# A two-layer attention trunk on one core: value products for two pairs of heads at a time, and up products grouped by the rounded and the remainder part of the weights

## The chip, the core and the metric

The kernel runs on one core of a Trainium2 chip. A core has engines that work side by side and each take their instructions in a fixed order: TensorE (PE in the profile, with its weight loads as PEld), VectorE (DVE), ScalarE (ACT), GpSimd (POOL, unused here but for a few instructions) and SyncE (SP), which issues the DMA transfers from HBM. Matmul results go to PSUM, which has eight banks of 512 float32 columns on each of 128 partitions; VectorE and ScalarE read them from there. The metric is the time of one execution in device microseconds, the median of several runs.

## The reference

Two layers work on 256 tokens of width 1024. Each layer is a mixer and an MLP, both between norms:

```
h   = rms_norm(x, g_pre_mix);  parts = h @ w_in
o   = concat(nsa(parts), fox(parts));  x += rms_norm(o @ w_out, g_post_mix)
h   = rms_norm(x, g_pre_mlp)
y   = square(relu(h @ w_up)) @ w_down;  x += rms_norm(y, g_post_mlp)
```

`nsa` has 8 query heads in 2 groups that share keys and values. Each head has three outputs (compressed, selected and window attention), and their gated sum is its result. At 256 tokens all blocks are selected and the window covers everything before the token, so selected and window attention are both causal softmax attention, over different keys and values. Compressed attention has 15 keys, made from the tokens by a small network. `fox` has 8 heads of causal softmax attention with a forgetting term added to the logits. All of it is float32.

## The kernel before

**Products in three parts.** TensorE multiplies a rounded float32 type faster than full float32. Each weight that arrives from HBM (`wraw`) is split into a rounded part `whi` (ScalarE) and a remainder `wlo` (VectorE), and activations are split in the same way. A product then is `hi*hi + hi*lo + lo*hi`, three matmuls into the same PSUM columns (`mm3`). Softmax probabilities and values stay in full float32, and so do transposes.

**An order made by a planner.** Almost all instructions are recorded first (`Recorder`), so that they have one source line in the profile, L350, where they are emitted. The planner (`order`, from line 243) then plays the recording with costs for each operation and decides in which order each engine takes its work: the one with the lowest key that is ready, where keys follow the order of recording. A group inside `nc.stretch()` stays together on TensorE. Buffers are part of this: an operation whose tile has no free buffer waits, and tiles of one tag get theirs in the order of recording. The order is fixed when the program is built; on the chip each engine follows it and waits on semaphores.

**The mixer.** The columns of `w_in` are computed in six chunks (c0 to c5). Attention runs in a loop over `flat` (lines 1237 to 1273): 16 steps for NSA (four pairs of heads, two heads a pair, selected and window branch) and 8 for fox. In this pipeline each iteration does the scores of step i (TensorE, then on VectorE the mask and row extremes, on ScalarE the exponentials), scales those of step i-1 (`scale`, VectorE), transposes those of step i-2 (`probs_T`: three TensorE transposes into a PSUM bank of tag "s" and a copy to the tile `prT`, by VectorE and ScalarE in turn), and multiplies with the values what was ready at step i-3 (`pv`). Between these, `fill` takes pieces of a stream of other TensorE work: the chunks c1 to c5, then the products with `w_out` of the first four 128-row slices.

**Value products.** `pv` runs once for each pair of heads, when both heads (and, for NSA, both branches) are there: 4 NSA pairs and 4 fox pairs in a layer. For a pair it has a PSUM bank of tag "o" (there is one), of which it uses 256 columns; one head's output goes to partitions 0 to 63, the other's to 64 to 127. Each matmul has 64 columns of values as weights, so two run beside each other in two halves of the array. NSA has two terms (selected `vS`, window `vW`), fox has one (`fV`). For NSA a full-width matmul adds the compressed branch of the pair (`vbig`, `pcT`). `o_evac` then splits the 256 columns into the rounded and remainder tiles `oT` (tags act0 and act1, two buffers each, which the MLP uses for its activations).

**The MLP.** The hidden width of 4096 is worked on in 8 slices of 512. The first (`up0`) is computed by tokens. The other seven (`up`, line 1319) are computed transposed in four blocks of 128 hidden rows: 8 steps over the input width with, in each, a 512-wide matmul of `whi` with both parts of `xT` side by side and a 256-wide matmul of `wlo` with the rounded part, which is added to the upper 256 columns. Two layers of seven slices of four blocks make 56 blocks. Each slice is followed by the down products of the slice before it, into four PSUM banks (tags "x" and "acc").

The functions that the diff touches:

Of the kernel before, what the change touches and what calls it, by code (L numbers as in the profile page):

```python
# [18 lines left out]
F32 = mybir.dt.float32  # L19
# [5 lines left out]
P = 128  # L25
D = 1024
S = 256
NT = 2
DEPTH = 2
HD = 64  # L30
# [430 lines left out]
def trunk(nc, A, consts_in, out, sbp, pp):  # L461
    def tile(shape, dtype, name, tag=None, bufs=1):
        return nc.tile(sbp[(tag or name) not in OPERANDS], shape, dtype, name, tag, bufs)

    def psum(tag):
        return nc.tile(pp, [P, 512], F32, tag, tag, {"acc": 2, "x": 2, "s": 3, "o": 1}[tag], psum=True)

    def small(shape, name, bufs=2):
        return tile(shape, F32, name=name, tag=name, bufs=bufs)
# [18 lines left out]
    for l in range(DEPTH):  # L488
        w_in = A["w_in"][l].rearrange("(k p) n -> p k n", p=P)
        for c, (a, b) in enumerate(CHUNKS):  # L490
            for q, (k0, k1) in enumerate(parts_of(l, c)):
                add_unit((l, "in", c, q), [k1 - k0, b - a], w_in[:, k0:k1, a:b])
                if (c, q) in RIDES:
                    s, j = RIDES[c, q]
# [24 lines left out]
    def weight(*key):  # L519
        return W.get(index[key])  # L520
# [55 lines left out]
    def load_gains(*rows):  # L576
        g = tile([P, 2, D], F32, name="gains", tag="gain")
        for i, (name, l) in enumerate(rows):
            nc.sync.dma_start(g[:, i, :], A[name][l].partition_broadcast(P))
        return [g[:, i, :] for i in range(2)]  # L580
# [23 lines left out]
    def split(src, dst):  # L604
        nc.scalar.activation(dst[0], src, AF.Copy)
        nc.vector.tensor_sub(dst[1], src, dst[0].bitcast(F32))
# [123 lines left out]
    for l in range(DEPTH):  # L730
# [12 lines left out]
        vS, vW, fV, gate = ([None] * 2 for _ in range(4))  # L743
        gates = small([P, NT, 24], "gate")
        T = {}
        oT = {}
# [301 lines left out]
        done = set()  # L1048
# [23 lines left out]
        def fill(n):  # L1072
            for _ in range(n):
                if step() in ("wait", "end"):
                    return
# [33 lines left out]
        def scores(e):  # L1109
            kind, pair, par, br = e[:4]  # L1110
            if kind == "fox":
                if par == 0:
                    T["sc"] = fox_scores(pair)
                ps = T["sc"][par]
            else:
                if br == 1:
                    T["sc"] = nsa_scores(e)
                ps = T["sc"][br - 1]
            p = small([P, 384], "pr", 3)
            st = small([P, 4], "st", 4)  # L1120
            for a, b, t in SEGS:
                nc.vector.tensor_tensor_reduce(
                    out=p[:, a:b], in0=ps[t], in1=cst[:, C_MASK + 256 - (b - a):C_MASK + 256], op0=OP.add, op1=OP.min,
                    scale=-0.125, scalar=3.0e38, accum_out=st[:, t:t + 1])
            for a, b, t in SEGS:
                nc.scalar.activation(p[:, a:b], p[:, a:b], AF.Exp, scale=-1.0, bias=st[:, t:t + 1],
                                     accum_out=st[:, 2 + t:3 + t])
            return p, st

        def scale(e, p, st):  # L1130
            kind, pair, par, br = e[:4]
            nc.vector.reciprocal(st[:, 2:4], st[:, 2:4])
            for a, b, t in SEGS:
                if kind == "fox":
                    nc.vector.tensor_scalar(p[:, a:b], p[:, a:b], st[:, 2 + t:3 + t], None, op0=OP.mult)
                else:
                    c = 3 * (2 * pair + par) + br
                    nc.vector.tensor_scalar(p[:, a:b], p[:, a:b], st[:, 2 + t:3 + t], gate[t][:, c:c + 1],
                                            op0=OP.mult, op1=OP.mult)

        def probs_T(p, eng):
            ps = psum("s")
            for a in (0, 128, 256):
                nc.tensor.transpose(ps[:, a:a + P], p[:, a:a + P], ident)
            pT = small([P, 384], "prT", 6)
            if eng:
                nc.scalar.activation(pT, ps[:, :384], AF.Copy)
            else:
                nc.vector.tensor_copy(pT, ps[:, :384])
            return pT  # L1150

        def pv(o, terms, last):

            with nc.stretch():
                for i, (pT, V, cols) in enumerate(terms):
                    for kb in range(2):
                        for par in range(2):
                            h = slice(par * HD, par * HD + HD)
                            c = cols[par]
                            if kb == 0:  # L1160
                                nc.tensor.matmul(o[h, 0:S], V[0][:, c:c + HD], pT[par][:, 0:S],
                                                 start=i == 0, stop=False, skip_group_check=True)
                            else:
                                nc.tensor.matmul(o[h, P:S], V[1][:, c:c + HD], pT[par][:, S:S + P],
                                                 start=False, stop=last and i == len(terms) - 1, skip_group_check=True)

        def o_evac(o, kind, pair):
            if (kind, 0) not in oT:
                for j in range(2):
                    oT[kind, j] = tile([P, 4, S], F32R, name="oT", tag=f"act{j}", bufs=2)  # L1170
            split(o[:, :S], [oT[kind, j][:, pair, :] for j in range(2)])
            done.add(("o", pair + (0 if kind == "nsa" else 4)))


        if first:
# [61 lines left out]
        flat = [("nsa", pair, par, br) for pair in range(4) for par in range(2) for br in (1, 2)]  # L1237
# [4 lines left out]
        st = {}  # L1242
        pTs = {}
        o = None
        nc.lane = len(nc.ops)
        for i in range(len(flat) + 4):
            if 0 <= i - 1 < len(flat):
                scale(flat[i - 1], *st[i - 1])
            if i < len(flat):
                st[i] = scores(flat[i])  # L1250
                if i == 15:
                    done.add("nsa")
                    g_post, g_pre2 = load_gains(("g_post_mix", l), ("g_pre_mlp", l))
            fill(1)
            if i in side:
                side[i]()
                fill(1)
            if 0 <= i - 2 < len(flat):
                pTs[flat[i - 2]] = probs_T(st.pop(i - 2)[0], i % 2)
            fill(1)  # L1260
            j = i - 3
            if 0 <= j < len(flat) and flat[j][2] == 1 and flat[j][3] != 1:
                kind, pair, par, br = flat[j]
                o = psum("o")
                cols = [(pair // 2) * HD] * 2 if br else [2 * pair * HD, 2 * pair * HD + HD]
                pv(o, [([pTs.pop((kind, pair, x, b)) for x in range(2)], (fV, vS, vW)[b], cols)
                       for b in ((1, 2) if br else (0,))], not br)
                if br:
                    nc.tensor.matmul(o[:, :S], T["vbig"][:, pair].rearrange("p j d -> p (j d)"), T["pcT"],
                                     start=False, stop=True, skip_group_check=True)  # L1270
                o_evac(o, kind, pair)
            if i >= 12 or i % 2:
                fill(1)

# [44 lines left out]
        def up(fc, then=None):  # L1319
            a = [tile([P, 4, S], F32R, name="aT", tag=f"act{j}", bufs=2) for j in range(2)]  # L1320
            for b in range(4):
                hi, lo = weight(l, "up", fc, b)

                ps = psum("s")
                for k in range(8):
                    nc.tensor.matmul(ps, hi[:, k, :], xT[2][:, k].rearrange("p j n -> p (j n)"), start=k == 0, stop=False,
                                     skip_group_check=True)
                    nc.tensor.matmul(ps[:, S:], lo[:, k, :], xT[0][:, k, :], start=False, stop=k == 7,
                                     skip_group_check=True)
                if then is not None and b == 1:  # L1330
                    then()
                if b % 2 == 0:
                    h = tokt("h")
                d = h[:, (b % 2) * S:(b % 2) * S + S]
                nc.scalar.activation(d, ps[:, S:], AF.Copy)
                nc.vector.tensor_add(d, ps[:, :S], d)
                if b % 2:
                    rl = small([P, 512], "rl")
                    nc.scalar.activation(rl, h, AF.Relu)
                    nc.vector.tensor_mul(h, rl, rl)  # L1340
                    d = [y[:, b - 1:b + 1, :].rearrange("p b n -> p (b n)") for y in a]
                    nc.scalar.activation(d[0], rl, AF.Square)
                    nc.vector.tensor_sub(d[1], h, d[0].bitcast(F32))
            return a
# [41 lines left out]
        act, then = up0()  # L1386
        for fc in range(8):
# [12 lines left out]
            if fc < 7:  # L1400
# [5 lines left out]
                act = nxt  # L1406
# [59 lines left out]
```

## Time and profile before

| | |
|---|---|
| median of 3 runs | 635.33 us (635.32 to 635.46) |
| the profiled execution | 635.77 us, of which the span of instructions is 634.0 us |
| PE busy | 625.5 us (99%), 3570 matmuls |
| PEld busy (weight loads) | 520.4 us (82%) |
| DVE busy | 480.9 us (76%) |
| ACT busy | 373.8 us (59%) |
| granted clock of TensorE | 0.998 |
| HBM read | 114.07 MB |

Attention lies at about 56 to 126 us in the first layer and 368 to 437 us in the second; the seven transposed up slices and their down products fill most of the time between 150 and 315 us and between 460 and 615 us. In the page, a group of instructions has its engine, its operation, the tiles it writes and reads, its shape, how often it occurs, its busy time, and the mean length of one in ns. Matmuls overlap with the next, so their length is more than their share of the time; the distance from one start to the next is that share. In the timeline, neighbouring instructions of one group are merged into one row with a count.

### The profile page before, as it was taken

Reading aid. Unit: us, or ns where it says so; the run is one execution under the profiler, and the core shown is the slowest. Engines: PE = TensorE matmul, PEld = TensorE weight load, DVE = VectorE, ACT = ScalarE, POOL = GpSimd, SP = SyncE. Lnnn points to the kernel's source line nnn. Section 1 sums busy time; section 2 is a strip of 40 time slices with the busy share of each in tenths; the row PEclk is TensorE's granted clock in tenths of the full one; section 3 lists DMA queues with packets and bytes.
Section 4 is the critical chain, followed back from the end, with each engine's and each line's share of the span. In section 5 each row is a group of like instructions: output and inputs, shape, how many; then the busy total and the mean of one; then the engine's idle time right before and its main releaser. Section 6 shows DMA issues by size and latency. Waiting matters only on the chain.

```text
span 634.0 us, 9913 instructions
## 1 busy us (share of the span) xinstructions
PE 625.5 (99%) x3570; PEld 520.4 (82%) x3570; DVE 480.9 (76%) x1084; ACT 373.8 (59%) x737; POOL 0.2 (0%) x4
## 2 busy tenths in 40 slices
PE   9999999999999999999999999999999999999995
PEld 6888977688888888888888988777888888888884
DVE  6899998869985665566598999987998665666544
ACT  7865676564864455456467656864658464455432
POOL 0000000000000000000000000000000000000000
PEclk9999999999999999999999999999999999999999
DMA  8998436225786666656329954432267766655601
GB/s 307 345 321 284 131 100 168 85 67 174 247 280 196 196 178 197 194 185 183 121 81 308 331 167 130 166 101 67 66 230 259 228 184 197 197 184 186 197 1 66
DMA packets 47005, 115.75 MB, mean 183 GB/s; under 512 B 4003, under 2 KB 14573, under 8 KB 46957
## 3 DMA queue, kind: packets, MB, share of 16 engines
q1 hardware_dynamic: 46956, 115.13, 56.8%
q8 instruction: 28, 0.46, 0.3%
q14 instruction: 21, 0.16, 0.1%
HBM read 114.07 MB, written 1.05 MB: 182 GB/s over the span
## 4 chain that ended last, share of the span: by engine, by line
PE 98%; DMA 1%; DVE 0%; ACT 0%; SPq 0%; issue 0%; DVEq 0%
PE s L350 35%; PE acc L350 31%; PE x L350 25%; PE o L350 7%; DMA wraw<-in_w_in_dram 1%; SPq L350 0%; DVE x L350 0%; DVE m L350 0%; DVEq L1462 0%; ACT whi L350 0%; ACT xT L350 0%; DVE rsqrt L350 0%; ACT rl L350 0%; DVEq L350 0%
## 5 line engine op out<-in xcount | busy, mean ns | idle before, releaser
L350 DVE TENSOR_TENSOR wlo<-wraw,whi 128x1024 fp32r<-128x1024 f32 (+2 forms) x196 | 230.2, 1180 | 101.8 <-ACT whi L350 100.1
L350 ACT ACTIVATE whi<-wraw 128x1024 fp32r<-128x1024 f32 (+2 forms) x196 | 199.7, 1025 | 157.0 <-PE acc L350 74.2
L350 PE MATMUL s<-xT,whi 128*128 128x512 f32 x448 | 158.5, 397 | 0.0
L350 PE MATMUL s<-xT,wlo 128*128 128x256 f32 x448 | 125.7, 281 | 0.0
L350 PEld LDWEIGHTS s<-xT,whi 128*128 128x128 f32 x448 | 84.1, 188 | 20.5
L350 PE MATMUL acc<-whi,aT 128*128 128x512 f32 x256 | 88.9, 391 | 0.0
L350 PE MATMUL x<-whi,aT 128*128 128x512 f32 x256 | 88.8, 391 | 0.0
L350 PEld LDWEIGHTS s<-xT,wlo 128*128 128x128 f32 x448 | 84.6, 189 | 0.6
L350 PEld LDWEIGHTS x<-whi,aT 128*128 128x128 f32 x256 | 47.9, 188 | 10.2
L350 PEld LDWEIGHTS acc<-whi,aT 128*128 128x128 f32 x256 | 48.0, 188 | 10.0
L350 ACT ACTIVATE pr<-pr,st 128x128 f32<-128x128 f32 (+1 forms) x96 | 42.8, 447 | 17.5 <-DVE st L350 17.1
L350 PE MATMUL acc<-wlo,aT 128*128 128x512 f32 x128 | 49.9, 390 | 0.0
L350 PE MATMUL x<-wlo,aT 128*128 128x512 f32 x128 | 49.9, 390 | 0.0
L350 PE MATMUL acc<-xT,whi 128*128 128x256 f32 x256 | 49.4, 285 | 0.0
L350 PEld LDWEIGHTS acc<-xT,whi 128*128 128x128 f32 x256 | 40.4, 190 | 2.3 <-issue 1.4
L350 PE MATMUL x<-whi,xT 128*128 128x512 f32 x112 | 37.9, 408 | 0.5 <-ACT whi L350 0.3
L350 PE MATMUL acc<-whi,xT 128*128 128x512 f32 (+1 forms) x128 | 38.2, 359 | 0.0
L350 PE MATMUL acc<-xT,wlo 128*128 128x256 f32 x128 | 36.3, 286 | 0.0
L350 ACT ACTIVATE rl<-x 128x512 f32<-128x512 f32 x24 | 14.7, 612 | 24.9 <-PE x L350 16.8
L350 PEld LDWEIGHTS acc<-wlo,aT 128*128 128x128 f32 x128 | 24.0, 188 | 5.1
L350 PEld LDWEIGHTS x<-wlo,aT 128*128 128x128 f32 x128 | 24.0, 188 | 4.6
L350 ACT ACTIVATE h<-s 128x256 f32<-128x256 f32 x56 | 20.6, 368 | 10.7 <-PE s L350 10.7
(219 smaller groups left out, 963.2 us busy)
## 6 DMA issues: line engine op xcount, KB each, us to landing
wraw<-in_w_up_dram SPq DMA_DIRECT2D x64, 512.0 KB, 3.7
wraw<-in_w_down_dram SPq DMA_DIRECT2D x64, 512.0 KB, 3.9
wraw<-in_w_in_dram SPq DMA_DIRECT2D x39, 512.0 KB, 5.0
wraw<-in_w_out_dram SPq DMA_DIRECT2D x16, 512.0 KB, 3.6
w<-in_cmp_w_k_dram SPq DMA_DIRECT2D x8, 512.0 KB, 5.4
w<-in_cmp_w_v_dram SPq DMA_DIRECT2D x8, 512.0 KB, 8.2
wraw<-in_w_in_dram SPq DMA_DIRECT2D x8, 288.0 KB, 5.1
x<-in_x_dram SPq DMA_DIRECT2D x4, 256.0 KB, 7.4
```

What stands on the lines that cost most here:

```text
L350: getattr(getattr(self.nc, op.engine), name)(*[real(v) for v in args], **{k: real(v) for k, v in kw.items()})
```

## The change

Two edits that don't touch each other.

Value products: `pv` now takes two pairs. At the even pair nothing is done; at the odd pair one group holds the matmuls of both, the even pair in columns 0 to 255 of the bank, the odd pair in columns 256 to 511, and only the first matmul of each partition half clears the bank. The two `vbig` matmuls follow it, and one evacuation of 512 columns fills two slices of `oT`. The even pair's `prT` tiles are thus held until the odd pair is ready; for the odd NSA pairs the transposed probabilities go to a new tile `prX` in the buffers of tags act0 and act1.

Up products: in each block the eight 512-wide matmuls with `whi` come first, then the eight 256-wide ones with `wlo`; the number and the operands are the same.

```diff
-        def probs_T(p, eng):
+        def probs_T(p, eng, e):
             ps = psum("s")
             for a in (0, 128, 256):
                 nc.tensor.transpose(ps[:, a:a + P], p[:, a:a + P], ident)
-            pT = small([P, 384], "prT", 6)
+            kind, pair, par, br = e
+            if kind == "nsa" and pair % 2:
+                if br == 1:
+                    T["prX"] = tile([P, 4, S], F32, name="prX", tag=f"act{par}", bufs=2).rearrange("p b n -> p (b n)")
+                pT = T["prX"][:, (br - 1) * 384:br * 384]
+            else:
+                pT = small([P, 384], "prT", 6)
...
-        def pv(o, terms, last):
+        def pv(o, pairs, last):
             with nc.stretch():
-                for i, (pT, V, cols) in enumerate(terms):
+                for q, terms in enumerate(pairs):
+                    for i, (pT, V, cols) in enumerate(terms):
...
-                                nc.tensor.matmul(o[h, 0:S], V[0][:, c:c + HD], pT[par][:, 0:S],
-                                                 start=i == 0, stop=False, skip_group_check=True)
+                                    nc.tensor.matmul(o[h, q * S:q * S + S], V[0][:, c:c + HD], pT[par][:, 0:S],
+                                                     start=q == 0 and i == 0, stop=False, skip_group_check=True)
...
-            split(o[:, :S], [oT[kind, j][:, pair, :] for j in range(2)])
+            split(o.rearrange("p (b n) -> p b n", b=2), [oT[kind, j][:, pair - 1:pair + 1, :] for j in range(2)])
...
-                o = psum("o")
...
+                if pair % 2:
+                    o = psum("o")
...
+                    if br:
+                        for q in range(2):
+                            nc.tensor.matmul(o[:, q * S:q * S + S], T["vbig"][:, pair - 1 + q].rearrange("p j d -> p (j d)"),
+                                             T["pcT"], start=False, stop=True, skip_group_check=True)
+                    o_evac(o, kind, pair)
...
                 for k in range(8):
                     nc.tensor.matmul(ps, hi[:, k, :], xT[2][:, k].rearrange("p j n -> p (j n)"), start=k == 0, stop=False,
                                      skip_group_check=True)
+                for k in range(8):
                     nc.tensor.matmul(ps[:, S:], lo[:, k, :], xT[0][:, k, :], start=False, stop=k == 7,
                                      skip_group_check=True)
```

More of the change, by code (lines that the diff above doesn't have):

```diff
@@ L1150, in probs_T @@
             return pT
-        def pv(o, terms, last):
+        def pv(o, pairs, last):
             with nc.stretch():
-                for i, (pT, V, cols) in enumerate(terms):
[L1156 to L1160, printed above, removed]
-                                nc.tensor.matmul(o[h, 0:S], V[0][:, c:c + HD], pT[par][:, 0:S],
-                                                 start=i == 0, stop=False, skip_group_check=True)
-                            else:
-                                nc.tensor.matmul(o[h, P:S], V[1][:, c:c + HD], pT[par][:, S:S + P],
-                                                 start=False, stop=last and i == len(terms) - 1, skip_group_check=True)
+                for q, terms in enumerate(pairs):
+                    for i, (pT, V, cols) in enumerate(terms):
+                        for kb in range(2):
+                            for par in range(2):
+                                h = slice(par * HD, par * HD + HD)
+                                c = cols[par]
+                                if kb == 0:
+                                    nc.tensor.matmul(o[h, q * S:q * S + S], V[0][:, c:c + HD], pT[par][:, 0:S],
+                                                     start=q == 0 and i == 0, stop=False, skip_group_check=True)
+                                else:
+                                    nc.tensor.matmul(o[h, q * S + P:q * S + S], V[1][:, c:c + HD], pT[par][:, S:S + P],
+                                                     start=False, stop=last and i == len(terms) - 1,
+                                                     skip_group_check=True)
         def o_evac(o, kind, pair):
@@ L1170, in o_evac @@
                     oT[kind, j] = tile([P, 4, S], F32R, name="oT", tag=f"act{j}", bufs=2)
-            split(o[:, :S], [oT[kind, j][:, pair, :] for j in range(2)])
-            done.add(("o", pair + (0 if kind == "nsa" else 4)))
+            split(o.rearrange("p (b n) -> p b n", b=2), [oT[kind, j][:, pair - 1:pair + 1, :] for j in range(2)])
+            for x in (pair - 1, pair):
+                done.add(("o", x + (0 if kind == "nsa" else 4)))
         if first:
@@ L1258, in trunk @@
             if 0 <= i - 2 < len(flat):
-                pTs[flat[i - 2]] = probs_T(st.pop(i - 2)[0], i % 2)
+                pTs[flat[i - 2]] = probs_T(st.pop(i - 2)[0], i % 2, flat[i - 2])
             fill(1)
@@ L1263, in trunk @@
                 kind, pair, par, br = flat[j]
-                o = psum("o")
[L1265 to L1271, printed above, removed]
+                if pair % 2:
+                    o = psum("o")
+                    cols = lambda q: [(q // 2) * HD] * 2 if br else [2 * q * HD, 2 * q * HD + HD]
+                    pv(o, [[([pTs.pop((kind, q, x, b)) for x in range(2)], (fV, vS, vW)[b], cols(q))
+                            for b in ((1, 2) if br else (0,))] for q in (pair - 1, pair)], not br)
+                    if br:
[3 more added lines that the diff above has]
+                    o_evac(o, kind, pair)
             if i >= 12 or i % 2:
```

## The prediction

> **What bounds the kernel now.** I read the page first (share of each engine, chain of work), then the view of waits for TensorE alone, then the timeline of TensorE in the stages that the change touches.
>
> ```profile
> span 634.0 us, 9913 instructions
> ...
> PE 625.5 (99%) x3570; PEld 520.4 (82%) x3570; DVE 480.9 (76%) x1084; ACT 373.8 (59%) x737; POOL 0.2 (0%) x4
> ...
> PE 98%; DMA 1%; DVE 0%; ACT 0%; SPq 0%; issue 0%; DVEq 0%
> ...
> L350 PE MATMUL s<-xT,wlo 128*128 128x256 f32 x448 | 125.7, 281 | 0.0
> ...
> L350 PEld LDWEIGHTS s<-xT,wlo 128*128 128x128 f32 x448 | 84.6, 189 | 0.6
> ```
>
> ```profile
> PE o L350 <- DVE warm L350: 1.2, 1, 1.2
> PE x L350 <- ACT whi L350: 0.3, 1, 0.3
> PE x L350 <- ACT xT L350: 0.2, 1, 0.2
> ```
>
> TensorE (PE) carries 98% of the chain that ends last, and the second fence is everything it waited for: 1.7 us of 634. So the time is the sum of the distances from one matmul's start to the next one's. A busy figure does not give that distance, because matmuls overlap (281 ns "of one" in the group row is longer than its slot); the timeline does. Whatever the change takes out of those distances comes off the end, unless PE must then wait for something.
>
> **Change 1, the order in the up products.** Each of 56 blocks (28 a layer; 448 / 8) has eight 512-wide matmuls on rounded weights and eight 256-wide on remainders. They alternate now; after the change eight of one kind precede eight of the other. Nothing is added or removed. The rows are TensorE's timeline (start, length, operation, how many were merged): a stretch of down products with 512 columns alone, then four alternating up blocks.
>
> ```profile
> 495.41 0.40 PE L350 MATMUL acc<-whi,aT 128*128 128x512 f32 x1
> ...
> 504.95 0.39 PE L350 MATMUL s<-xT,whi 128*128 128x512 f32 x1
> 505.17 0.28 PE L350 MATMUL s<-xT,wlo 128*128 128x256 f32 x1
> 505.29 0.40 PE L350 MATMUL s<-xT,whi 128*128 128x512 f32 x1
> ...
> 516.24 0.40 PE L350 MATMUL x<-whi,aT 128*128 128x512 f32 x1
> ```
>
> From 495.41 to 504.95 there are 42 matmuls of 512 columns: 9.54 / 42 = 0.2271 us each. From 504.95 to 516.24 there are 32 alternating pairs: 11.29 / 32 = 0.3528 us a pair. The price of 256 columns among their own kind is in the forget-query products of layer 0, where only such matmuls follow each other:
>
> ```profile
> 63.83 0.40 PE L350 MATMUL acc<-xT,whi 128*128 128x256 f32 x2
> ...
> 65.63 0.63 PE L350 MATMUL x<-kx,qS 128*128 128x512 f32 x2
> ...
> 66.10 0.39 PE L350 MATMUL acc<-xT,whi 128*128 128x256 f32 x2
> ...
> 68.83 0.29 PE L350 MATMUL acc<-xT,wlo 128*128 128x256 f32 x1
> ```
>
> Fifteen steps in 1.80 us and 23 in 2.73: 4.53 / 38 = 0.1192 us. So a pair costs 0.3528 - 0.2271 - 0.1192 = 0.0065 us more in alternation than its two parts do apart: the price of two changes of width. A block keeps one such pair of changes and loses seven: 7 x 0.0065 x 56 = 2.5 us. Every weight is needed at the same time as now or later: the block starts on rounded weights, which are one tile and are already all needed at its first matmul, and the remainders, which VectorE (DVE) makes, are first read eight matmuls in, not one. I therefore add no wait. The bounds of this part: a gain of 2.5 if the slots are as quoted; a loss if remainders in a row are paced by their weight loads, whose row says 189 ns: 7 x (0.189 - 0.119) x 56 = 27 us lost. I take the first, because the 256-wide stream above loads weights for each matmul too and still steps at 0.119.
>
> **Change 2, probabilities times values for two pairs at once.** Now there are 16 groups of such products (8 a layer), each holding PE in a mode with 64 output columns; after, 8 groups of double length. The matmuls in them are the same in number and size. What goes is eight changes into the mode and eight out of it. One NSA group (two terms a pair) and one forget group (one term):
>
> ```profile
> 72.81 0.63 PE L350 MATMUL x<-kx,qS 128*128 128x512 f32 x2
> 73.37 0.87 PE L350 MATMUL o<-prT,vS 128*64 128x256 f32 x8
> 74.07 0.82 PE L350 MATMUL o<-prT,vW 128*64 128x256 f32 x8
> 74.82 0.50 PE L350 MATMUL acc<-xT,whi 128*128 128x256 f32 x2
> 75.16 0.28 PE L350 MATMUL acc<-xT,wlo 128*128 128x256 f32 x1
> ```
>
> ```profile
> 125.42 0.39 PE L350 MATMUL x<-whi,oT 128*128 128x512 f32 x1
> 125.74 0.87 PE L350 MATMUL o<-prT,fV 128*64 128x256 f32 x8
> 126.54 0.50 PE L350 MATMUL x<-whi,oT 128*128 128x512 f32 x1
> 126.88 0.40 PE L350 MATMUL x<-wlo,oT 128*128 128x512 f32 x1
> ```
>
> Two terms take 74.82 - 73.37 = 1.45 us, one takes 126.54 - 125.74 = 0.80, so a term alone is 0.65 and 0.15 of each group is fixed. The matmul before it is late in giving way: 73.37 - 72.81 = 0.56 for two that cost 0.454 elsewhere (0.10), 0.32 instead of 0.227 (0.09). The one after it as well: 0.34 for two 256-wide ones that cost 0.238 (0.10), 126.88 - 126.54 = 0.34 instead of 0.227 (0.11). Together 0.15 + 0.10 + 0.10 = 0.35 us a group; eight groups fewer give 2.8 us.
>
> The product of compressed probabilities (o<-pcT,vbig) follows each NSA pair, eight in all. In the built order before, three of them stand between rounded-type matmuls; after, all eight stand as four twos behind transposes of probabilities, which are of the same unrounded type.
>
> ```profile
> 93.66 0.48 PE L350 MATMUL acc<-wlo,xT 128*128 128x512 f32 x1
> 93.97 0.59 PE L350 MATMUL o<-pcT,vbig 128*128 128x256 f32 x2
> ```
>
> The step into one is 0.31 instead of 0.227: 0.09 each, three times, 0.3 us.
>
> Evacuation of the outputs: 16 of 256 columns become 8 of 512 on ScalarE (ACT) and on DVE. The groups by form give the sizes:
>
> ```profile
> L350 DVE TENSOR_TENSOR oT<-o,oT 128x256 fp32r<-128x256 f32 x16 | 6.7, 419 | 2.2 <-ACT oT L350 2.2
> L350 ACT ACTIVATE oT<-o 128x256 fp32r<-128x256 f32 x16 | 6.0, 374 | 7.0 <-PE o L350 7.0
> L350 DVE TENSOR_TENSOR xT<-s,xT 128x512 fp32r<-128x512 f32 x12 | 8.2, 691 | 2.6 <-ACT xT L350 2.5
> L350 ACT ACTIVATE xT<-s 128x512 fp32r<-128x512 f32 x12 | 7.1, 598 | 4.1 <-PE s L350 3.9
> ```
>
> By the xT rows of the same form, DVE saves 6.7 - 8 x 0.691 = 1.2 us and ACT 6.0 - 8 x 0.598 = 1.2 us. Both lie beside PE and I count nothing. One evacuation lasts longer (0.598 + 0.691 = 1.29 us against 0.79), which matters behind the last group of a layer, where out products of its pairs follow. In the built order four other matmuls (0.9 us) stand between that group and the first that needs its rounded part, so I cost this at nothing; with the cover gone it costs at most 0.5 us a layer.
>
> What is queued behind the long group: while PE does 2 x 1.3 + 0.15 = 2.75 us of value products it makes no scores and no transposes, which DVE lives on. The stages of layer 0 (PE busy, PEld, DVE, ACT, with counts):
>
> ```profile
> 70.00:84.00 14.00, 14.00 (x101) 11.76 (x99) 13.57 (x61) 9.86 (x31) 0.00 (x0) 1.00 0.28 95
> 84.00:98.00 14.00, 14.00 (x97) 10.53 (x95) 13.53 (x54) 10.69 (x36) 0.00 (x0) 1.00 0.51 142
> 98.00:112.00 14.00, 14.00 (x86) 10.32 (x85) 11.23 (x38) 9.27 (x25) 0.00 (x0) 1.00 0.54 162
> ```
>
> DVE has 0.43 and 0.47 us to spare in 14 where the NSA pairs run and 2.77 in the next stage. The new order fills the long groups with splits of weights on DVE (wlo), which have to be done anyway, so I cost this at zero; the loss end is the longer hold itself: 1.30 us at four NSA groups and 0.65 at four forget groups, 7.8 us.
>
> The odd pairs' transposed probabilities go to a new tile in the act0 and act1 buffers. The copies keep their size and engine; these buffers are unused by then in layer 0, and in layer 1 their readers, the last down products of layer 0, are long past. On SP's queue of loads one step moves: in layer 0 the two gain loads, issued at 91.77, come behind one more load of out weights and one of up weights.
>
> ```profile
> 91.77 0.33 SPq L350 DMA_DIRECT2D gains<-in_g_post_mix_dram  x1
> ...
> 94.38 0.33 SPq L350 DMA_DIRECT2D wraw<-in_w_out_dram  x1
> 97.84 40.80 SPq L350 DMA_DIRECT2D wraw<-in_w_up_dram  x8
> ```
>
> At worst they go out after the first of the loads from 97.84, six microseconds late, while their first reader on DVE stands 12 instructions further on (12 x 13.53 / 54 = 3 us), so it would wait 3 us; at best they go out when they do now, since the two loads ahead wait for weight splits that the new order puts earlier. I take zero, as PE has fill matmuls for such a gap. Nothing moves on POOL.
>
> **The sum.** -2.5 - 2.8 - 0.3 = -5.6 us. The profiled execution took 635.77 us (span 634.0 and 1.8 around it): 630.2. Its time is 0.44 above the median of the runs, so the median should come to 635.33 - 5.6 = 629.7 us.
>
> **The rivals.** *Order does not matter:* the 6.5 ns belong to the up products themselves (their operands), not to the change of width, and stay. For it: the price is a difference of three rows from three places. Against it: the operands are laid out as in those rows. Then only change 2 pays: 635.33 - 3.1 = 632.2. The Trainium skill ("TensorE: Matmul & The Clock Gate", section "Back-to-back issue gap") has such a rule for the plain matmul: a gap of N / 2.4 + 2.5 ns, whatever stands beside it. By it a pair would cost 325 ns in either order and change 1 would give nothing; the trace has 352.8, so the rule does not hold to the 7 ns in question here.
>
> *DVE runs dry (slower):* each long group delays scores and transposes, DVE falls behind by the longer hold, and PE, once its fill is used up, waits for transposed probabilities. Place: the matmuls right behind each double group. Price: up to 7.8 us, 635.33 - 5.6 + 7.8 = 637.5. It decides once 70% of the hold comes back as PE waits (5.6 of 7.8). For it: the DVE rows at 97%. Against it: the weight splits that fill the gap, and the 2.77 us of the next stage. Half of it would give 633.6.
>
> *Remainders paced by their loads (slower):* 27 - 3.1 is 24 us more, 659. It decides from a slot of 0.119 + 5.6 / 392 = 0.133 us for a 256-wide matmul in a row (392 = 7 x 56). For it: 189 ns a load, and that in the 256-wide stream two of three matmuls reload the same weights. Against it: the third does not, and no step there stands out.
>
> **How the numbers follow.** The sum as worked out 0.60 (its own range 628.4 to 631.2: half a microsecond of late evacuation a layer above, 1.3 us of better slots below). Order does not matter 0.12. DVE dry by half 0.06, by about all of the gain (no change) 0.07, beyond it 0.11. Loads 0.04. A measurement of this kernel can tell about 0.2% (1.3 us) from no change. Faster: 0.60 + 0.12 + 0.06 = 0.78; same 0.07; slower 0.15. The range 627.6 to 635.4 holds the first three and most of the fourth; below it reaches 0.8 us past the first's own range for a dearer mode change than the two groups shown.
>
> **What would show it.** In the profile after: the up blocks at 8 x 0.227 + 8 x 0.119 + 0.007 = 2.78 us where four took 11.29 (2.82 each); eight groups in the 64-column mode, NSA ones near 2.75 us and forget ones near 1.45; the view of PE's waits still under 3 us. A PE wait for prT, prX or pr behind a double group shows the second rival; a 256-wide step over 0.133 us shows the third; up blocks still at 2.82 show the first. The prediction is wrong if PE waits for more than 4 us in the attention stages, or if the long groups cost more inside than their terms.

## The result, and the profile after

The changed kernel takes 630.87 us (median of 4 runs, 630.74 to 631.18) against 635.39 for the kernel before beside it (635.32 to 635.72): a ratio of 0.9928, 95% interval 0.9914 to 0.9942. That is 4.5 us less, where 5.6 were forecast; the time lies inside both ranges of the prediction.

From the page of the changed kernel (span, busy time of the engines, shares of the chain, one group: busy us, mean ns of one, idle before), and from its view of TensorE's waits (engine and tile, what it waited for, us in total, times, longest):

```profile
span 629.0 us, 9910 instructions
...
PE 619.7 (99%) x3570; PEld 521.0 (83%) x3570; DVE 480.8 (76%) x1076; ACT 373.4 (59%) x729; POOL 0.2 (0%) x4
...
PE 95%; DVE 1%; ACT 1%; DMA 1%; SPq 0%; issue 0%; DVEq 0%; ACTq 0%
...
L350 PE MATMUL s<-xT,wlo 128*128 128x256 f32 x448 | 62.5, 282 | 0.0
```

```profile
PE o L350 <- DVE warm L350: 1.2, 1, 1.2
PE acc L350 <- DVE fkT L350: 0.5, 1, 0.5
PE x L350 <- ACT whi L350: 0.4, 1, 0.4
PE x L350 <- ACT xT L350: 0.2, 1, 0.2
```

TensorE is still the chain (95%) and waits for 2.3 us in all. Two things are to be seen. The group of narrow up matmuls fell from 125.7 us busy to 62.5 with the same 448 matmuls, while the whole kernel gained 4.5: a group's busy time counts overlap with its neighbours, so regrouping halves it and says nothing of a gain. And one wait is new: `acc` for DVE's `fkT`.

Where the time went is read from the starts of three matmuls: the first wide one of the up products of layer 0, the first of layer 1 (288 columns) and the first wide up matmul of layer 1. TensorE's timeline of before, then of after:

```profile
149.44 0.39 PE L350 MATMUL s<-xT,whi 128*128 128x512 f32 x1
...
329.74 0.29 PE L350 MATMUL acc<-whi,xT 128*128 128x288 f32 x1
...
460.20 0.39 PE L350 MATMUL s<-xT,whi 128*128 128x512 f32 x1
```

```profile
147.43 1.98 PE L350 MATMUL s<-xT,whi 128*128 128x512 f32 x8
...
326.65 0.29 PE L350 MATMUL acc<-whi,xT 128*128 128x288 f32 x1
...
456.27 1.98 PE L350 MATMUL s<-xT,whi 128*128 128x512 f32 x8
```

With the first 288-column matmul of layer 0 (17.83 us before, 17.68 after) and the span's end, these cut the span into four stages, the ruler for everything below. A row is one profiled execution; a stage is the difference of two starts in us:

| kernel | mixer of layer 0 | MLP of layer 0 | mixer of layer 1 | MLP of layer 1 to the end |
|---|---|---|---|---|
| before | 131.62 | 180.30 | 130.46 | 173.78 |
| changed | 129.75 | 179.21 | 129.63 | 172.69 |
| up products alone | 131.36 | 179.21 | 130.49 | 172.69 |
| value products alone | 129.63 | 180.29 | 129.64 | 173.91 |
| compressed product between | 130.87 | 179.24 | 130.53 | 172.71 |
| early bank | 129.16 | 179.23 | 129.05 | 172.69 |
| four and four | 129.77 | 179.75 | 129.62 | 173.19 |
| zigzag | 129.72 | 179.21 | 129.91 | 172.68 |
| forget pairs alone in twos | 130.63 | 179.22 | 129.80 | 172.69 |
| NSA pairs alone in twos | 130.29 | 179.23 | 130.68 | 172.68 |
| changed, again | 129.72 | 179.22 | 129.61 | 172.70 |
| early bank, again | 129.62 | 179.22 | 129.19 | 172.68 |
| zigzag and early bank | 129.78 | 179.22 | 129.05 | 172.68 |

The MLP stages repeat within 0.03 us among kernels with the same up order (0.13 in the second one of before's order; more on it under change 1 below). The mixer of layer 0 does not: the early bank gives 129.16 and 129.62 in two executions, and 129.78 with the zigzag, where TensorE also waits 0.37 us for a load. So changed less before is -1.87 and -0.83 in the mixers and -1.09 and -1.09 in the MLPs, -4.88 together; the rest of the 5.0 between the spans lies ahead of the first of these matmuls.

### The profile page after: what moved, and what is told of

It is laid out like the page before. It is cut to its first block, busy times and chain, and to the rows that moved or that the text cites. A ratio compares the mean times of both kernels' runs of the same rounds, so it can differ in the third digit from the quotient of the medians.

```text
span 629.0 us, 9910 instructions
## 1 busy us (share of the span) xinstructions
PE 619.7 (99%) x3570; PEld 521.0 (83%) x3570; DVE 480.8 (76%) x1076; ACT 373.4 (59%) x729; POOL 0.2 (0%) x4
## 4 chain that ended last, share of the span: by engine, by line
PE 95%; DVE 1%; ACT 1%; DMA 1%; SPq 0%; issue 0%; DVEq 0%; ACTq 0%
PE s L350 35%; PE acc L350 30%; PE x L350 23%; PE o L350 7%; DMA wraw<-in_w_in_dram 1%; ACT whi L350 0%; SPq L350 0%; ACT rl L350 0%; DVE wlo L350 0%; ACT xT L350 0%; DVE pr L350 0%; DVE fkT L350 0%; DVE x L350 0%; DVE m L350 0%; DVEq L1476 0%
## 5 line engine op out<-in xcount | busy, mean ns | idle before, releaser
L350 PE MATMUL s<-xT,whi 128*128 128x512 f32 x448 | 112.0, 392 | 0.0
L350 PEld LDWEIGHTS s<-xT,whi 128*128 128x128 f32 x448 | 81.4, 189 | 15.2
L350 PEld LDWEIGHTS s<-xT,wlo 128*128 128x128 f32 x448 | 61.1, 190 | 4.4
L350 PE MATMUL s<-xT,wlo 128*128 128x256 f32 x448 | 62.5, 282 | 0.0
L350 PE MATMUL acc<-whi,xT 128*128 128x512 f32 (+1 forms) x128 | 36.2, 355 | 0.5 <-DVE fkT L350 0.5
L350 ACT ACTIVATE rl<-h 128x512 f32<-128x512 f32 x28 | 17.4, 623 | 16.1 <-DVE h L350 16.1
```

Of the source, the lines that this page charges most:

```text
L350: getattr(getattr(self.nc, op.engine), name)(*[real(v) for v in args], **{k: real(v) for k, v in kw.items()})
```

## The experiments

Each ratio is to the kernel before, run beside it; the median of before was 635.56 us for the first four below; 635.39 for the changed kernel and the early bank side by side and for the NSA pairs alone; and 635.72 for the other four.

### Each edit alone

The up products alone, on the kernel before:

```diff
                 for k in range(8):
                     nc.tensor.matmul(ps, hi[:, k, :], ...)
+                for k in range(8):
                     nc.tensor.matmul(ps[:, S:], lo[:, k, :], ...)
```

> The kernel before with the grouped up products alone. Theory A (the two edits add up; the landmarks of the two MLPs moved by -1.06 us each): 2.1 us below before, 633.3, up blocks at 2.79 us each. Theory B (the prediction's term): 2.5 us below, 632.9, blocks at 2.78. Theory C (order does not matter, the gain in the MLP came with the value products): within 0.3 us of before, blocks at 2.82.

Measured: 633.29 us, ratio 0.9965 (0.9952 to 0.9977), 2.3 us less. The table has -1.09 in each MLP and nothing in the mixer of layer 1, 2.2 us in all: nearest to theory A; theory C falls. (B's 2.5 lies inside the interval too; it is the table that speaks against it. The 0.26 us in the mixer of layer 0, which the edit doesn't touch, is within what that stage varies.)

The value products alone, from the changed kernel:

```diff
-                for k in range(8):
                     nc.tensor.matmul(ps[:, S:], lo[:, k, :], ...)
```

> The changed kernel with the alternating order of up products put back, so the double value groups alone. Theory A (what the traces show for the two attention stages): 2.4 us below before, 633.0, with about 0.8 us of PE lost behind the evacuation fkT of the fourth chunk. Theory B (the prediction's term): 3.1 us below, 632.3. Theory C (all of the gain is from the value products): 4.5 us below, 630.9.

Measured: 633.39 us, ratio 0.9966 (0.9953 to 0.9978), 2.2 us less; in the table -1.99 and -0.82 in the mixers, nothing gained in the MLPs. That is nearest to theory A, and C falls: each edit gains in its own stage, the two add up (2.3 + 2.2 = 4.5), and neither brings it all. B's 3.1 lies just outside the interval (about 1.4 to 3.0).

### What a way into the 64-column mode and out of it costs

The order is changed so that each NSA double group is left once in its middle, for a product that is there anyway and is of the same unrounded type:

```diff
                                     nc.tensor.matmul(o[h, q * S + P:q * S + S], V[1][:, c:c + HD], ...)
+                    if not last:
+                        nc.tensor.matmul(o[:, q * S:q * S + S], T["vbig"][:, vpair - 1 + q]..., T["pcT"], ...)
...
-                        for q in range(2):
-                            nc.tensor.matmul(o[:, q * S:q * S + S], T["vbig"][:, pair - 1 + q]..., T["pcT"], ...)
```

> The changed kernel, but in each of the four NSA double groups the compressed product of a pair comes right behind that pair's selected and window products, so PE leaves the 64-column mode and enters it again once more in the middle of each group; all matmuls the same. Theory A (a way into the mode and out of it costs 0.35 us, whatever stands between): 4 x 0.35 = 1.4 us above the changed kernel. Rival (the price belongs to the change between rounded and unrounded operands, which the compressed product does not have): within 0.3 us of the changed kernel.

Measured: 632.99 us, ratio 0.9959 (0.9946 to 0.9971): 2.6 us below before where the changed kernel is 4.5 below, so about 1.9 above it. TensorE's timeline of the changed kernel around one NSA double group and one forget group, then of this one around an NSA double group:

```profile
85.22 0.87 PE L350 MATMUL o<-prT,vS 128*64 128x256 f32 x8
85.92 0.82 PE L350 MATMUL o<-prT,vW 128*64 128x256 f32 x8
86.57 0.82 PE L350 MATMUL o<-prX,vS 128*64 128x256 f32 x8
...
87.97 0.44 PE L350 MATMUL s<-cst,pr 128*128 128x128 f32 x2
88.24 1.03 PE L350 MATMUL o<-pcT,vbig 128*128 128x256 f32 x4
89.11 0.49 PE L350 MATMUL s<-cst,pr 128*128 128x128 f32 x3
...
114.84 1.52 PE L350 MATMUL o<-prT,fV 128*64 128x256 f32 x16
116.30 0.50 PE L350 MATMUL acc<-whi,oT 128*128 128x512 f32 x1
```

```profile
396.75 0.82 PE L350 MATMUL o<-prT,vW 128*64 128x256 f32 x8
397.50 0.70 PE L350 MATMUL o<-pcT,vbig 128*128 128x256 f32 x2
398.13 0.87 PE L350 MATMUL o<-prX,vS 128*64 128x256 f32 x8
398.83 0.82 PE L350 MATMUL o<-prX,vW 128*64 128x256 f32 x8
399.58 0.70 PE L350 MATMUL o<-pcT,vbig 128*128 128x256 f32 x2
400.11 0.71 PE L350 MATMUL s<-cst,pr 128*128 128x128 f32 x5
```

In the undisturbed group the second term steps in 86.57 - 85.92 = 0.65 us, and the compressed products take 89.11 - 88.24 = 0.87 for two. Left in the middle, the term ahead takes 0.75 (396.75 to 397.50), the compressed product 0.63 instead of 0.43, and the first term of the second pair 0.70 instead of 0.65: 0.10 + 0.20 + 0.05 = 0.35 us, the price in the prediction, with no change of operand type in it. So the rival falls: the 64-column mode has this price. (The Trainium skill, "TensorEngine Tiling (Array Packing)", section "Key Properties", says that a change of tiling mode drains the engine and gives no price; the 0.35 us in and out are in keeping with it, though no row shows the draining itself.) At the group's end the compressed product loses 0.10 where transposes had lost 0.05, so a group costs 0.39 more and four 1.6; the remaining 0.3 us (0.5 by the two mixers of the table, 1.1 and 0.9 longer) came with an order that differs at other places too, and was not followed up.

### The evacuation that lost its cover

In the changed kernel TensorE's timeline has this at the start of chunk c5, in layer 0 and in layer 1; below it DVE's timeline in layer 1:

```profile
74.07 0.28 PE L350 MATMUL acc<-xT,wlo 128*128 128x256 f32 x1
74.42 0.50 PE L350 MATMUL acc<-whi,xT 128*128 128x512 f32 x1
...
382.77 0.28 PE L350 MATMUL acc<-xT,wlo 128*128 128x256 f32 x1
383.50 0.50 PE L350 MATMUL acc<-whi,xT 128*128 128x512 f32 x1 [0.46 <-DVE fkT L350]
```

```profile
381.64 1.21 DVE L350 TENSOR_TENSOR wlo<-wraw,whi 128x1024 fp32r<-128x1024 f32 x1
382.76 1.29 DVE L350 TENSOR_TENSOR fkT<-acc,rT 128x512 f32<-128x512 f32 x2
```

The steps are 0.35 and 0.73 us where 0.12 is usual. The first bank of c4 must be evacuated (`fkT`) before c5 writes into it, and DVE reaches that only after a split of weights. In the kernel before, the value products of the first NSA pair stood between the last matmuls of c4 and covered it (TensorE's timeline, then DVE's, of before):

```profile
385.59 0.87 PE L350 MATMUL o<-prT,vS 128*64 128x256 f32 x8
...
387.04 0.39 PE L350 MATMUL acc<-xT,wlo 128*128 128x256 f32 x1
...
387.50 0.28 PE L350 MATMUL acc<-xT,wlo 128*128 128x256 f32 x1
387.62 0.40 PE L350 MATMUL acc<-whi,xT 128*128 128x512 f32 x1
```

```profile
385.85 0.68 DVE L350 TENSOR_TENSOR fkT<-acc,rT 128x512 f32<-128x512 f32 x1
```

The group ran from 385.59 to 387.04, `fkT` at 385.85 beside it, and c5 followed after 0.12 us. To test this, the cover is made unnecessary: the last part of c3's and c4's products finishes the first bank before it turns to the second.

```diff
-                for k in range(k0, k1):
-                    for b in range(4):
+                for k, b in ([(k, b) for b2 in (0, 2) for k in range(k0, k1) for b in (b2, b2 + 1)] if k1 == 8 else
+                             [(k, b) for k in range(k0, k1) for b in range(4)]):
```

> The changed kernel, but the last part of the chunk products of c3 and c4 finishes the first PSUM bank before it goes on with the second, so that the evacuation fkT of the first bank can start some 0.7 us earlier. Theory A (the pair-0 value group that went away had covered this evacuation): the steps into the next chunk's first matmul fall from 0.73 us (layer 1) and 0.35 us (layer 0) to 0.12, 0.6 to 0.8 us below the changed kernel. Rival (the wait only moves on, as DVE ends the same work at the same time): within 0.2 us of the changed kernel.

Measured: 629.91 us, ratio 0.9919 (0.9906 to 0.9933), 5.6 us below before where the changed kernel is 4.5 below. TensorE's timeline and DVE's, layer 1:

```profile
382.30 0.28 PE L350 MATMUL acc<-xT,wlo 128*128 128x256 f32 x1
382.42 0.40 PE L350 MATMUL acc<-whi,xT 128*128 128x512 f32 x1
```

```profile
381.18 0.69 DVE L350 TENSOR_TENSOR fkT<-acc,rT 128x512 f32<-128x512 f32 x1 [0.26 <-PE acc L350]
...
382.13 1.21 DVE L350 TENSOR_TENSOR wlo<-wraw,whi 128x1024 fp32r<-128x1024 f32 x1
```

`fkT` now comes ahead of the split, and the step is 0.12, in layer 0 too. To see whether this reaches the end, the changed kernel and this one ran side by side once more:

> The changed kernel itself beside the next one on the same chip: 4.5 us below before, 631.1.

> The version with the early bank beside the changed kernel on the same chip. If the 0.85 us of the two steps reach the end: 0.8 to 1.1 us below the changed kernel. If they are taken back later: within 0.3 us of it.

Measured: 631.22 us, ratio 0.9928 (0.9916 to 0.9941), and 630.42 us, ratio 0.9917 (0.9904 to 0.9931). The medians are 0.80 apart and the intervals overlap; the two steps (0.23 + 0.62 = 0.85) and the table's mixer of layer 1 (129.61 against 129.05 and 129.19) say that it is a gain. In layer 0 the step falls by 0.23 us too, but that mixer varies by more, and the table doesn't show whether it reaches the end there. Alone or with the zigzag below it is the fastest version here.

### Which groups lost the cover

Only the forget pairs in twos, then only the NSA pairs (the core of the edit; the second has `"nsa"` in its place):

```diff
-                if pair % 2:
+                both = kind in ("fox",)
+                if pair % 2 or not both:
+                    qs = (pair - 1, pair) if both else (pair,)
```

> The changed kernel with the value products of forget pairs in twos and those of NSA pairs one pair at a time as before; the NSA products of the first pair stand again before the first matmul of c5. Theory A (0.35 us a group, and the pair-0 group covers the evacuation fkT): the way through attention costs 4 x 0.35 = 1.4 us less than with single groups everywhere, the step into c5's first matmul is 0.12 us again; together with the up products 1.4 + 2.1 = 3.5 us below before, 632.0. Rival (forget groups gain nothing, as the extra hold of 0.65 us makes PE wait behind them): 2.1 below, 633.4.

> The changed kernel with the value products of NSA pairs in twos and those of forget pairs one pair at a time as before. Theory A (0.35 us a group, 0.3 us for compressed products no longer between rounded ones, and the lost cover of fkT): 1.4 + 0.3 - 0.7 = 1.0 us through attention, with the up products 2.1 more: 3.1 us below before, 632.5, and the waits behind fkT in both layers as in the changed kernel. Rival (the lost cover comes from the moved forget groups): no wait at c5, 3.8 below, 631.8.

Measured: forget pairs 632.46 us, ratio 0.9947 (0.9935 to 0.9960), 3.3 less; NSA pairs 632.45 us, ratio 0.9951 (0.9939 to 0.9964), 2.9 less. TensorE's timeline of the first, then of the second:

```profile
386.16 0.28 PE L350 MATMUL acc<-xT,wlo 128*128 128x256 f32 x1
386.28 0.40 PE L350 MATMUL acc<-whi,xT 128*128 128x512 f32 x1
```

```profile
383.66 0.28 PE L350 MATMUL acc<-xT,wlo 128*128 128x256 f32 x1
384.38 0.50 PE L350 MATMUL acc<-whi,xT 128*128 128x512 f32 x1 [0.44 <-DVE fkT L350]
```

With the first pair's group back, the step is 0.12; with NSA pairs in twos it is 0.72. Against the kernel with the up products alone, forget pairs gain 0.73 and 0.69 in the two mixers (4 x 0.35 = 1.4 forecast), NSA pairs gain 1.07 in layer 0 and lose 0.19 in layer 1, 0.9 in all (1.0 forecast). Theory A holds for both in the total, and for the forget pairs by layer. For the NSA pairs the same sum gives 0.7 in layer 0 and 0.2 in layer 1, so there the total fits better than its parts: the lost cover takes back 0.62 us in layer 1, and 0.4 more is not explained.

### What the alternation of wide and narrow matmuls costs

TensorE's timeline of the changed kernel, four up blocks:

```profile
500.83 1.98 PE L350 MATMUL s<-xT,whi 128*128 128x512 f32 x8
502.64 1.11 PE L350 MATMUL s<-xT,wlo 128*128 128x256 f32 x8
503.59 2.00 PE L350 MATMUL s<-xT,whi 128*128 128x512 f32 x8
505.43 1.12 PE L350 MATMUL s<-xT,wlo 128*128 128x256 f32 x8
...
511.97 0.40 PE L350 MATMUL x<-whi,aT 128*128 128x512 f32 x1
```

A block is (511.97 - 500.83) / 4 = 2.785 us; the prediction had 2.78. The first eight wide matmuls, behind down products that are wide too, take 502.64 - 500.83 = 1.81 us, the next block's eight, behind narrow ones, 505.43 - 503.59 = 1.84. In a run of their own kind wide ones step at 226.7 ns and narrow ones at 120. Averaged over the second and the fourth block of the slices, the eight wide ones step 233, 236, 228, 232, 231, 227, 227, 227 ns, and the narrow ones 113, 119, then 120; over all 56 a block is 2.790 us (2.817 in the kernel before). So the wide ones are late by 27 ns behind a run of narrow ones, spread over five matmuls, and the first two narrow ones are early by 7 to 8: a return to wide costs some 20 ns net, not the 6.5 of the prediction. Behind the last block of a slice the down products, wide too, are late in the same way: 48 of them take 10.943 us before and 10.907 after, 63 and 27 ns more than 48 steps of 226.7. All steps of an MLP stage in layer 0 summed by kind: up products 78.88 us before and 78.11 after, down products 87.95 and 87.63, the rest 13.47 and 13.48. Two experiments vary how many of a kind follow each other. Four and four:

```diff
                 for k in range(8):
                     nc.tensor.matmul(ps, hi[:, k, :], ...)
-                for k in range(8):
-                    nc.tensor.matmul(ps[:, S:], lo[:, k, :], ...)
+                    if k % 4 == 3:
+                        for m in range(k - 3, k + 1):
+                            nc.tensor.matmul(ps[:, S:], lo[:, m, :], ...)
```

> The changed kernel with up blocks of four wide, four narrow, four wide, four narrow matmuls. Theory A (each return from narrow to wide costs about 21 ns, however many narrow ones came before, as after a run of eight): two returns a block, 2.81 us a block, 56 x 0.021 = 1.2 us above the changed kernel. Theory B (the price grows with each narrow matmul and is paid back later, so eight narrow ones cost the same in one run or in two): 2.79 us a block, within 0.3 us of the changed kernel. Theory C (the prediction's 6.5 ns for two changes of width): 0.0065 x 56 = 0.36 us above.

Measured: 632.23 us, ratio 0.9944 (0.9932 to 0.9957): 3.5 us below before, 1.0 above the changed kernel's 4.5. The table has +0.54 and +0.50 in the MLPs. And the zigzag, in which every second block does its narrow matmuls first:

```diff
                 for k in range(8):
-                    nc.tensor.matmul(ps, hi[:, k, :], ...)
+                    if b % 2:
+                        nc.tensor.matmul(ps[:, S:], lo[:, k, :], ...)
+                    else:
+                        nc.tensor.matmul(ps, hi[:, k, :], ...)
```

> The changed kernel, but every second up block does its narrow matmuls first, so that runs of sixteen narrow and sixteen wide ones follow each other and returns to wide matmuls are halved. Theory A (21 ns a return): 28 x 0.021 = 0.6 us below the changed kernel. Theory B (price by narrow matmuls): within 0.2 us. Theory C (6.5 ns for two changes of width): 0.2 us below.

Measured: 631.21 us, ratio 0.9930 (0.9916 to 0.9943), 4.5 us below before: no gain, and the MLPs in the table are the changed kernel's to 0.01 us. TensorE's timeline with four and four, from inside a block, then the zigzag's in the first slice of layer 0:

```profile
503.21 1.09 PE L350 MATMUL s<-xT,whi 128*128 128x512 f32 x4
504.14 0.63 PE L350 MATMUL s<-xT,wlo 128*128 128x256 f32 x4
```

```profile
150.08 0.63 PE L350 MATMUL x<-whi,aT 128*128 128x512 f32 x2
150.66 1.22 PE L350 MATMUL s<-xT,wlo 128*128 128x256 f32 x8
```

Four wide ones behind narrow ones take 504.14 - 503.21 = 0.93 us instead of 4 x 0.2267 = 0.907: as late as the first four of eight. That is theory A's kind, with a net price of 20 ns: 28 more returns a layer are 0.56 us, and the table has 0.54 and 0.50.

By that price the zigzag should save 14 x 0.020 = 0.28 us a layer, 0.04 a slice. In the slices behind the first it does: four blocks with the down products behind them take 22.013 us, in the changed kernel 22.053. In the first slice of each layer it loses as much, 0.23 us: there the planner's order has two down products between the first two runs of narrow matmuls (150.08 in the rows), where the changed kernel has none. They take 150.66 - 150.08 = 0.58 us instead of 0.453, and the eight narrow ones behind them 1.06 (to 151.72) instead of 0.95. Why these are slow was not followed up. So the result is B's number, but theory A's price holds in the other slices, and the zigzag's order was not given its own test without those two down products. Theory C falls with both: four and four lost 1.0 us where it has 0.36, and the zigzag's twelve other slices gain 0.48 where it has 0.16. What makes the wide ones late is open; weight loads of 190 ns against narrow steps of 120 would fit a lag that the wide ones work off, but no run here shows it.

The early bank and the zigzag together, both diffs in one kernel:

> The changed kernel with both the early bank of the chunk products and the up blocks in zigzag. Theory A (the two savings add): 0.85 + 0.6 = 1.4 to 1.7 us below the changed kernel, about 629.3. If zigzag brings nothing: as with the early bank alone, 629.9.

Measured: 630.31 us, ratio 0.9913 (0.9900 to 0.9927), 5.4 below before, as the early bank alone (5.6 and 5.0 in its two runs): the zigzag adds nothing here either; its two down products stand in the first slices here too.

## Why the prediction was right, and where it was off

**What bounds the kernel.** Right: TensorE's steps were the time, and what came out of them came off the end.

**Change 1.** The effect and its place were right, the term a little too large: 2.5 forecast, 2.2 measured (1.09 in each MLP, and 2.3 with the edit alone). The step that failed is the factor 56 in "7 x 0.0065 x 56": a price read from one stretch was put on every block. It holds behind the first slice of each layer: there four blocks and the down products behind them take 22.233 us before and 22.053 after, 0.18 less, which is 28 x 6.4 ns. The first slice fell by 0.02 only (22.513 to 22.493), so twelve slices gave 2.16 us and two 0.03. In the kernel before, two down products stand in the first block of that slice, and the 47 up matmuls behind them alternate without a surcharge. TensorE's timeline of layer 1, before, then with the value products alone, where all matmuls of this stage stand in the same order:

```profile
464.16 0.28 PE L350 MATMUL s<-xT,wlo 128*128 128x256 f32 x1
...
472.25 0.39 PE L350 MATMUL x<-wlo,aT 128*128 128x512 f32 x1
```

```profile
461.76 0.28 PE L350 MATMUL s<-xT,wlo 128*128 128x256 f32 x1
...
470.00 0.40 PE L350 MATMUL x<-wlo,aT 128*128 128x512 f32 x1
```

Before, they take 8.09 us, (8.09 - 0.12) / 23 = 0.3465 a pair, which is 0.2267 + 0.120; with the value products alone 8.24, 0.353 a pair, the price of the other slices. That is the 0.13 us by which the MLP of layer 1 differs between the two in the table. So alternation can run at either pace, and the order does not decide which; what does is open. The size within a slice was partly luck as well: counted with the down products behind them, 32 returns cost 0.26 us before, 8 ns each, and the four that are left 0.08, 20 each, where the prediction had 6.5 for both; the two errors cancel. Of the 2.2 us, 1.5 lie in the up products and 0.6 in the down products behind them, a place that was not in the sum.

The rival that order does not matter is refuted by the run with the up products alone. The Trainium skill ("TensorE: Matmul & The Clock Gate", section "Back-to-back issue gap") gives N / 2.4 + 2.5 ns for the gap of a single matmul, by the page's own words an isolated one, which the prediction left out; that is 216 ns for 512 columns. The trace has 227 and more behind narrow ones, so the formula does not describe this stream. Remainders paced by their loads are refuted too: narrow steps in a row are 0.120 us, below the 0.133 from which it would have decided.

**Change 2.** The price of 0.35 us a group was right: double NSA groups took 2.75 us (85.22 to 87.97), a forget group 1.46 (114.84 to 116.30), as worked out, and leaving a group in its middle costs 0.35 inside it. All eight compressed products do stand behind transposes, so the 0.3 us stands as far as the rows go. Of the 3.1 us, 2.2 were measured by the medians with the edit alone, and the table's mixers have 2.5 to 2.8, by which of the kernels with single groups they are set against. The term missing from the sum is the evacuation of c4's first bank: 0.23 + 0.62 us of waiting, of which 0.12 in layer 0 was there before: 0.73 net, and 3.1 - 0.73 = 2.4. With the early bank, which removes that wait, the three executions have mixers 3.0 to 3.6 us below those of the up products alone, in keeping with the 3.1. The step that failed is "eight groups fewer give 2.8 us": it counted the group of the first pair only as a cost to be removed, and didn't ask what it had covered. The prediction did look for what comes late, but behind the double groups ("what is queued behind the long group") and not at the place that a group leaves.

**DVE runs dry.** Refuted: the kernel became faster, and no wait for `prT`, `prX` or `pr` is in the view of waits. DVE stays as full as before (the view by stages gives 13.55 and 13.65 of 14 us in the first two stages of layer 0), which is as the prediction had it, with weight splits to fill the time.

**Costed at nothing.** The longer evacuations, the transposed probabilities in the act0 and act1 buffers and the gain loads moved on SP's queue show no wait of TensorE in the view of waits.

**The chances.** The likeliest case came true, in part by luck: its range of 628.4 to 631.2 us allowed half a microsecond a layer for a late evacuation of the outputs behind the last group, and what came late was another evacuation, by 0.12 and 0.62 us. The 0.73 us of lost cover and the 0.3 us too much in the up products make up 1.0 of the 1.2 us between 629.7 and 630.87.

## What to carry to other kernels

Before work is taken off the bounding engine or moved, look at what ran beside it on the other engines: an evacuation that it covered becomes a wait, and here that took back 0.73 of 3.1 us until the matmuls ahead were ordered so that the bank came free earlier. Price an edit from starts to starts in the timeline, not from the busy time of a group, and make a ruler of stages that hold one edit each, so that each term of a sum can be checked. Where only 6 ns a matmul are at stake, read the price in every stretch that it will be multiplied by: here it held in twelve slices of fourteen, and the first of each layer had nothing to give.

## What the runs showed of the hardware that was not expected

Wide matmuls (512 columns) behind a run of narrow ones (256) are late for about five steps, by 27 ns in all behind eight, while the first narrow one behind wide ones steps 113 ns instead of 120: 20 ns a return, net. One wide and one narrow in turn run at either of two paces, 353 ns a pair or 346.5, the sum of the two parts, and the same matmuls in the same order took one in one kernel and the other in another (8.24 and 8.09 us for 47). A way out of the 64-column mode costs 0.05 us where transposes follow and 0.10 to 0.11 where rounded products or a compressed product do.
